# A Trainium2 backbone layer: x scaled by 1/rms while the modulation weights load, and a plain first tile in both feed-forwards

## Chip, cores and metric

One core of one Trainium2 chip. The metric is device time in microseconds (us), the median of several runs. A profile of one execution stands beside it, with its own time.

## What is computed

One layer of a diffusion backbone on 1024 latent tokens `x` and 256 context tokens `ctx`, width 1024, all in float32:

```python
m_x = silu(c) @ w_ada + b_ada          # nine modulations of 1024 for x; m_c from c_ctx for the context
x = x + 0.5 * m_x[2] * swiglu(modulate(rmsnorm(x, norm1_g), m_x[0], m_x[1]), ff1_in, ff1_out)
h = h + 0.5 * m_c[2] * swiglu(modulate(rmsnorm(h, norm1_g), m_c[0], m_c[1]), ff1_in, ff1_out)
x = x + m_x[5] * mixer(modulate(rmsnorm(x, norm2_g), m_x[3], m_x[4]), context states from h)
x = x + 0.5 * m_x[8] * swiglu(modulate(rmsnorm(x, norm3_g), m_x[6], m_x[7]), ff2_in, ff2_out)
return rmsnorm(x, final_g)
```

`modulate(x, shift, scale)` is `x * (1 + scale) + shift`; `swiglu` has 2816 hidden columns. The mixer joins gated linear attention and a spatial gate, and an output projection follows.

## The kernel before

Activations lie transposed: 8 tiles of 128 channels, `x[k][tb]`, with tb = 0 and 1 for two blocks of 512 tokens of x and tb = 2 for the context. Every precise product is made of three fp32r products (`hi*hi`, `hi*lo`, `lo*hi`); `hl` (L439 on) splits an operand into a high part on ScalarE (ACT) and a low part on VectorE (DVE). A plain fp32 matmul shows as two passes in the trace.

The big feed-forward products use a Winograd scheme over 2x2 blocks (`winograd`, L481 on): seven products (1 to 7) where plain blocks need eight. The right-hand operands `mov[1..7]` come from the four blocks of the normalized x: 1 and 2 are the upper and lower channels of the first token block; 5, 7, 6, 3 and 4 need the second block too. Each product is 12 instructions of 512 columns (L492); the context's part (`gc`, L539 to L541) has 256 columns. The weights of a tile f come through `unit` (L371 on): two loads into `raw` (two buffers), combinations on DVE, high and low parts in buffers with the tags `w` (six) and `m` (eight).

**The opening** (`run`): x of block 0 is loaded, then `ada_first` loads sixteen 512 KB tiles of modulation weights and multiplies each with two conditioning vectors into four PSUM banks (`row`, L206, two output rows each), copies them (L214) and turns them into columns with small products (`cols`, L216). Then come x of block 1 and the context. `rstd` squares on ACT (L305, L314), adds the eight squares up on DVE (L315), sums over channels with one-column products (`st`, L266) and takes 1/sqrt in 12 small DVE steps (L248 to L256, L280), once for each of the three blocks. `spread` (L289) copies 1/rms to all partitions by products into a PSUM bank `bc` (tag `pn`, two banks). `right_ops` (L447 on) multiplies x by its coefficient and by `bc` on DVE (L453), adds the shift on ACT (L454), and makes the operands. All this happens after the coefficients are known, block by block.

**Between the mixer and the second feed-forward** the mixer's last projection (`wo`, L357 to L360) adds to x one token block at a time; `done2(tb)` then normalizes that block and calls `right_ops`.

The order on each engine is set by the framework from the program's order, a simulated timeline and `high_priority` marks; each engine works its queue in that order. Loads go through SyncE's queue (SP).

Of the kernel before, what the change touches and what calls it, by code (L numbers as in the profile page):

```python
# [26 lines left out]
class Layer:  # L27
# [175 lines left out]
    def ada_rows(self, src, pr, i):  # L203
        wt = self.load(src[i], tag="d")
        for h in range(2):
            self.nc.tensor.matmul(pr[h][:2], self.sc[:, i, :], wt[:, h * 512:h * 512 + 512],  # L206
                                  start=(i == 0), stop=(i == NK - 1))

    def ada_cols(self, ch, pr):
        nc = self.nc  # L210
        row = self.m("row")
        pt = self.po("cols")
        for h in range(2):
            nc.scalar.activation(row[:2, h * 512:h * 512 + 512], pr[h][:2], AF.Copy)  # L214
            for dt in range(4 * h, 4 * h + 4):
                nc.tensor.matmul(pt[:, 2 * dt:2 * dt + 2], row[:2, dt * P:(dt + 1) * P], self.ident[:2, :2],  # L216
                                 start=True, stop=True)
        self.ada_bias(ch, 2, pt[:, :2 * NK].rearrange("p (k j) -> p k j", j=2))

    def ada_first(self):  # L220

        pr = [[self.po("row") for _ in range(2)], [self.pg("row") for _ in range(2)]]
# [61 lines left out]
    def spread(self, y, nt):  # L284

        nc = self.nc
        bc = self.pn("bc")
        for t in range(nt):
            nc.tensor.matmul(bc[:, t * P:(t + 1) * P], y[:, t:t + 1].to_broadcast([P, P]), self.ident,  # L289
                             start=True, stop=True)  # L290
        return bc
# [154 lines left out]

    def right_ops(self, tb, coef, bc, mov):  # L447

        nc = self.nc
        A, B = coef  # L450
        for k in (0, 4, 1, 5, 2, 6, 3, 7):
# [4 lines left out]
        def out(i, b, k):  # L456
            t = self.hl(b)
            mov[i][k] = t[:, :512], t[:, 512:]

        for k in range(4):  # L460
            if tb == 0:
                out(1, self.x[k][0], k)
                out(2, self.x[k + 4][0], k)
            else:
                (b11, b12), (b21, b22) = self.x[k][:2], self.x[k + 4][:2]
                self.combos(b11, b12, b21, b22, lambda i, b: out(i, b, k))
# [14 lines left out]
    def winograd(self, jobs):  # L481
# [24 lines left out]

        first(0)
        for j, job in enumerate(jobs):
            a, c, f = banks.pop(j), self.pg("c"), self.po("f")
            prod(c, job, 5)  # L510
            prod(f, job, 7)
            prod(a, job, 6, more=True)
            job[3].mid(a, c, f)
            if j + 1 < len(jobs):
                first(j + 1)
            prod(c, job, 3, more=True)
            prod(f, job, 4, more=True)
            job[3].end(c, f)

    def ffn(self, mov, yc, w1, w2, gates, load_x, load_c, tail, done, after_out=None):  # L520
# [14 lines left out]
        def plain(ps, parts, moving):  # L535

            n = len(parts)
            for i, ((hi, lo, c), (mh, ml)) in enumerate(zip(parts, moving)):
                nc.tensor.matmul(ps, hi[:, c], mh, start=i == 0, stop=False)  # L539
                nc.tensor.matmul(ps, hi[:, c], ml, start=False, stop=False)  # L540
                nc.tensor.matmul(ps, lo[:, c], mh, start=False, stop=i == n - 1)  # L541

        class Hidden:
# [3 lines left out]
            def ctx(s, i):  # L547
                w = s.w()
                rows = [(*w[r], slice(k * P, k * P + P)) for r in ((1, 2), (0, 4))[i] for k in range(4)]
# [3 lines left out]
                plain(ps, rows, yc)  # L553
# [9 lines left out]
                nc.sync.dma_start(hc[s.f // 2, :, h:h + 512], o.bitcast(F32))  # L563

# [63 lines left out]
        class Out:  # L628
# [4 lines left out]
            def ctx(s):  # L633
                w = s.w()
                ps = layer.po("oc")
                for i in range(2):
                    rows = [(*w[r], slice(s.col + k * P, s.col + k * P + P)) for r in ((1, 2), (0, 4))[i]
                            for k in range(s.kd)]
                    plain(ps[:, i * 256:i * 256 + 256], rows, s.right()["ctx"])
# [62 lines left out]
        def last():  # L702
# [3 lines left out]
                     for i in range(2)]  # L706
            rows = lambda w, i, col: [(*w[r], slice(col + k * P, col + k * P + P)) for r in ((1, 2), (0, 4))[i]
                                      for k in range(kd)]
            for tb in range(2):
# [6 lines left out]
                for m, i, w, col in tiles:  # L716
                    dt = m + 4 * i
                    ps = self.po("o") if i else self.pg("o")
                    plain(ps, rows(w, i, col), right)
# [8 lines left out]
            if yc:  # L728
# [6 lines left out]
                for m, i, w, col in tiles:  # L735
# [4 lines left out]
                    plain(ps, rows(w, i, col), right)  # L740
# [33 lines left out]
        self.winograd(jobs)  # L774
# [545 lines left out]
    def mixer(self, y, done=None):  # L1320
# [21 lines left out]
        for dt in range(NK):  # L1342
            w = self.wo_half(dt, 1, self.w)
            for tb in range(2):
                self.wo_add(w, bm[tb], dt, tb)
        ws = []
        ag = [self.gla_out(on[tb], tb) for tb in range(2)]
        for tb in range(2):
# [4 lines left out]
            if done:  # L1353
                done(tb)
# [22 lines left out]
    def run(self):  # L1377
# [11 lines left out]
        self.right_ops(0, c1, self.spread(rs[0], 4), mov)  # L1389
        y = ({}, {})  # L1390
        self.alloc_y(y, 2)
        self.norm(part(2), c1, y, rs[2])
        self.right_ops(1, c1, self.spread(rs[1], 4), mov)
# [23 lines left out]
        self.ffn(mov, yc, a["ff1i"], a["ff1o"], gates1, load_x1, lambda: self.load_c(self.d), self.squares(accs),  # L1417
# [16 lines left out]
        self.mixer(y2, done2)  # L1434
# [27 lines left out]
        self.ffn(mov, None, a["ff2i"], a["ff2o"], gates2, load_x2, None, self.squares(accs),  # L1462
# [81 lines left out]
```

## Time and profile before

| | |
|---|---|
| median of 3 runs | 2159.13 us (2155.48 to 2160.04) |
| the profiled execution | 2155.53 us, span 2153.8 us |
| TensorE (PE) busy | 2015.6 us, 94% |
| VectorE (DVE) busy | 1503.2 us, 70% |
| ScalarE (ACT) busy | 816.5 us, 38% |
| GpSimd (POOL) busy | 379.9 us, 18% |
| granted TensorE clock, mean | 0.968 |

Times in the profile count from the span's start. PE is the matmuls, PEld the weight loads beside them; matmuls are pipelined, so that the start of one after another tells their cost better than their length. A granted clock of 1.00 is 2.4 GHz, 0.50 is 1.2 GHz. In brackets stands how long an engine was idle before an instruction and what ended that.

### The profile page before, as it was taken

The numbers are of one execution on the slowest core, as the hardware profiler recorded it, in microseconds if no ns is written. First come the engines' busy times: TensorE is split into PE (matmuls) and PEld (weight loads), VectorE is DVE, ScalarE is ACT, GpSimd is POOL, SyncE is SP. The second block draws the span as 40 slices with busy tenths as digits, with TensorE's granted clock in tenths as the row PEclk, the third lists the DMA queues.
The fourth block names the chain that finished last, engine by engine and source line by source line (L and its number), as shares of the span: only waits on it lengthen the run. The fifth ranks groups of instructions, "written<-read, shape, count | busy, mean of one in ns | idle before, by whom it ended". The sixth has DMA issues, their size and how long they took to land.

```text
span 2153.8 us, 28445 instructions
## 1 busy us (share of the span) xinstructions
PE 2015.6 (94%) x10868; PEld 1669.6 (78%) x10868; DVE 1503.2 (70%) x2503; ACT 816.5 (38%) x1297; POOL 379.9 (18%) x215
## 2 busy tenths in 40 slices
PE   6799999999999999898999998787999999999997
PEld 1678888888887888787788877565888888868875
DVE  3976665656655779869888377778677786755585
ACT  3643333333333121256456345325343444442111
POOL 0000000000025555223210010300000000065740
PEclk9799999999999999999999899897999999999998
DMA  7033333333368786321111126550444343458742
GB/s 286 25 127 118 123 142 118 122 118 118 118 222 340 275 295 240 147 79 54 49 56 50 35 91 219 200 183 28 166 158 165 112 181 137 182 216 350 306 143 79
DMA packets 111273, 332.27 MB, mean 154 GB/s; under 512 B 12448, under 2 KB 15392, under 8 KB 111136
## 3 DMA queue, kind: packets, MB, share of 16 engines
q1 hardware_dynamic: 111136, 330.45, 41.8%
q8 instruction: 85, 1.39, 0.3%
q14 instruction: 52, 0.43, 0.1%
HBM read 231.31 MB, written 99.09 MB: 153 GB/s over the span
## 4 chain that ended last, share of the span: by engine, by line
PE 72%; DVE 18%; DMA 5%; issue 2%; ACT 2%; POOL 0%; SPq 0%; DVEq 0%; ACTq 0%
PE c L492 14%; PE a L492 14%; PE f L492 14%; PE b L492 7%; DVE acc L791 3%; DMA ar<-in_wb 2%; PE gc L541 2%; PE gc L540 2%; PE gc L539 2%; PE row L206 1%; DVE hl L444 1%; PE o L541 1%; PE o L539 1%; PE o L540 1%; DVE junk L169 1%
## 5 line engine op out<-in xcount | busy, mean ns | idle before, releaser
L384 POOL TENSOR_TENSOR s<-raw 128x512 f32<-128x512 f32 x18 | 23.8, 1322 | 1149.0 <-DVE ch L526 602.0
L169 DVE SCALAR_TENSOR_TENSOR junk<-ar,cr 128x512 bf16<-128x512 f32 x160 | 112.5, 703 | 58.6 <-DMA ar<-in_wb 44.1
L390 ACT ACTIVATE gh<-raw 128x1024 fp32r<-128x1024 f32 x62 | 65.7, 1059 | 171.6 <-PE c L492 64.1
L492 PE MATMUL f<-hl,uh 128*128 128x512 f32 x528 | 126.8, 389 | 0.0
L443 ACT ACTIVATE hl<-g 128x512 fp32r<-128x512 f32 x106 | 64.3, 626 | 157.4 <-DVE g L526 153.0
L492 PE MATMUL a<-hl,gh 128*128 128x512 f32 x352 | 114.4, 403 | 8.8 <-ACT hl L443 6.3
L492 PE MATMUL c<-hl,sh 128*128 128x512 f32 x352 | 111.1, 393 | 11.7 <-ACT hl L443 9.6
L394 ACT ACTIVATE sh<-s 128x1024 fp32r<-128x1024 f32 x62 | 65.5, 1057 | 147.1 <-PE a L492 87.1
L492 PEld LDWEIGHTS f<-hl,uh 128*128 128x128 f32 x528 | 99.1, 188 | 20.6
L492 PE MATMUL b<-hl,gh 128*128 128x512 f32 x352 | 112.3, 396 | 0.8 <-ACT hl L443 0.8
L492 PE MATMUL a<-hl,sh 128*128 128x512 f32 x352 | 110.1, 393 | 1.0 <-ACT g L567 1.0
L492 PE MATMUL f<-hl,th 128*128 128x512 f32 x352 | 110.2, 390 | 0.8 <-ACT hl L443 0.8
L492 PE MATMUL c<-hl,th 128*128 128x512 f32 x352 | 108.9, 391 | 0.0
L526 DVE TENSOR_TENSOR u<-c,u 128x512 f32<-128x512 f32 x44 | 30.2, 687 | 109.0 <-ACT u L577 109.0
L791 DVE SCALAR_TENSOR_TENSOR acc<-z,par,acc 128x945 f32<-128x945 f32 (+2 forms) x64 | 93.1, 1477 | 11.6 <-ACT acc L813 10.5
L143 POOL TENSOR_TENSOR wl<-raw,wh 128x1024 fp32r<-128x1024 f32 x20 | 52.0, 2606 | 257.5 <-ACT wh L142 257.2
L444 DVE TENSOR_TENSOR hl<-g,hl 128x512 fp32r<-128x512 f32 x106 | 74.9, 724 | 26.1 <-ACT hl L443 26.0
L492 PEld LDWEIGHTS c<-hl,sh 128*128 128x128 f32 x352 | 66.4, 189 | 27.4 <-ACT hl L443 10.2
L385 DVE TENSOR_TENSOR sl<-s,sh 128x1024 fp32r<-128x1024 f32 x44 | 54.8, 1246 | 45.2 <-PE gc L540 21.9
L492 PEld LDWEIGHTS a<-hl,gh 128*128 128x128 f32 x352 | 67.1, 195 | 23.0 <-ACT hl L443 6.8
L492 PEld LDWEIGHTS b<-hl,gh 128*128 128x128 f32 x352 | 67.3, 191 | 15.8 <-ACT hl L443 1.8
L492 PEld LDWEIGHTS a<-hl,sh 128*128 128x128 f32 x352 | 66.6, 189 | 15.7 <-ACT g L567 1.3
(342 smaller groups left out, 6030.6 us busy)
## 6 DMA issues: line engine op xcount, KB each, us to landing
hd<-hl SPq DMA_DIRECT2D x142, 512.0 KB, 3.6
hc<-hd SPq DMA_DIRECT2D x142, 512.0 KB, 7.4
ar<-in_wb SPq DMA_DIRECT2D x112, 256.0 KB, 3.1
raw<-in_ff1i SPq DMA_DIRECT2D x44, 512.0 KB, 3.7
raw<-in_ff2i SPq DMA_DIRECT2D x44, 512.0 KB, 4.5
raw<-in_ff1o SPq DMA_DIRECT2D x22, 512.0 KB, 4.9
raw<-in_ff2o SPq DMA_DIRECT2D x22, 512.0 KB, 4.8
x<-in_xT SPq DMA_DIRECT2D x16, 512.0 KB, 6.8
```

The source lines that it names most:

```text
L143: eng.tensor_tensor(out=lo[:, :n], in0=src[:, :n], in1=hi[:, :n].bitcast(F32), op=ALU.subtract)
L169: i = nc.vector.scalar_tensor_tensor(out=self.junk, in0=w, scalar=1.0, in1=cbc[j], op0=ALU.mult, op1=ALU.mult, accum_out=acc[:, h, dt, j:j ...
L385: sub = lambda o, x, y: eng.tensor_tensor(out=o, in0=x, in1=y, op=ALU.subtract)
L390: nc.scalar.activation(gh, g, AF.Copy)
L394: nc.scalar.activation(sh, s, AF.Copy)
L443: nc.scalar.activation(t[:, :512], src, AF.Copy)
L444: nc.vector.tensor_tensor(out=t[:, 512:], in0=src, in1=t[:, :512].bitcast(F32), op=ALU.subtract)
L492: mm = lambda x, y, start, stop: nc.tensor.matmul(ps, x, y, start=start, stop=stop, skip_group_check=more)
L539: nc.tensor.matmul(ps, hi[:, c], mh, start=i == 0, stop=False)
L540: nc.tensor.matmul(ps, hi[:, c], ml, start=False, stop=False)
L541: nc.tensor.matmul(ps, lo[:, c], mh, start=False, stop=i == n - 1)
L791: self.nc.vector.scalar_tensor_tensor(out=o, in0=zv[:, r0 + dr:r1 + dr, c0 + dc:c1 + dc], scalar=self.par[:, tap:tap + 1], in1=o, op0=ALU. ...
```

## The change

Four parts:

1. In `run` all of x and the context is loaded first, then the weights `w0` of the first feed-forward tile (`halves`, split at once), then the sixteen modulation weight tiles. While these load, `scaled` makes the squares of all three blocks, sums them with one-column products straight from the squares (only block 1 is added up on DVE first), takes 1/rms in one chain for all ten columns, spreads it and multiplies x by it in place.
2. In `ada_first` the rows' products go to one bank, in four groups of 32 partitions, and are ordered behind the last product of the spreading. The copies of the rows are split between ACT and DVE and ordered behind the last multiplication of x. The turn into columns uses four banks.
3. `right_scaled` makes the operands from the scaled x: scale and shift in one ACT instruction, operands 1, 2, 5, 3 first, then 7, 6, 4; operand 5 from the difference of the two blocks, which needs no shift. `right_ops`, kept for the second feed-forward, gets the same order.
4. The first tile of each feed-forward is computed plainly, with eight products for seven: `block0` needs operands 1 and 2 alone, then come products 1 and 2 of the next tile, then `block1` (operands 5 and 3). Its weights need no combinations. In the second feed-forward they are loaded and split (on POOL) ahead of the last projection's second group of weights.

```diff
-    def ada_first(self):
...
+    def ada_first(self, order):
+        nc = self.nc
+        pr = self.pg("row")
+        wts = [[self.load(self.a["wa"][ch, i], tag="d") for ch in range(2)] for i in range(NK)]
+        mm, order = order()
         for i in range(NK):
             for ch in range(2):
-                self.ada_rows(self.a["wa"][ch], pr[ch], i)
+                for h in range(2):
+                    g = 32 * (2 * ch + h)
+                    self.after(mm, nc.tensor.matmul(pr[g:g + 2], self.sc[:, i, :], wts[i][ch][:, h * 512:h * 512 + 512],
+                                                    start=(i == 0), stop=(i == NK - 1)))
+        row = self.h("row")
+        pts = [self.po("cols"), self.pg("cols"), self.po("cols"), self.pg("cols")]
         for ch in (1, 0):
-            self.ada_cols(ch, pr[ch])
+            for h in range(2):
+                q = 2 * ch + h
+                r = slice(32 * q, 32 * q + 2)
+                i = nc.scalar.activation(row[r], pr[r], AF.Copy) if h else nc.vector.tensor_copy(row[r], pr[r])
+                self.after(order, i)
+                for dt in range(4):
+                    nc.tensor.matmul(pts[q][:, 2 * dt:2 * dt + 2], row[r, dt * P:(dt + 1) * P], self.ident[r, r],
+                                     start=True, stop=True)
...
+    def right_scaled(self, coef, mov):
...
+        for k in range(4):
+            ds.append(self.h("dx"))
+            nc.vector.tensor_tensor(out=ds[k], in0=x[k][0], in1=x[k][1], op=ALU.subtract)
+        for k in range(4):
+            for i, kk in ((1, k), (2, k + 4)):
+                self.shift(x[kk][0], coef, kk)
+                self.right_op(mov, i, k, x[kk][0])
+        for k in range(4):
+            t = self.d("hl", F32R)
+            n = na[:, k:k + 1]
+            nc.scalar.activation(t[:, :512], ds[k], AF.Identity, scale=n)
+            nc.vector.scalar_tensor_tensor(out=t[:, 512:], in0=ds[k], scalar=n, in1=t[:, :512].bitcast(F32),
+                                           op0=ALU.mult, op1=ALU.subtract)
+            mov[5][k] = t[:, :512], t[:, 512:]
+        for k in range(4):
+            self.shift(x[k + 4][1], coef, k + 4)
+            self.right_op(mov, 3, k, x[k + 4][1])
...
+        plain.block0()
         first(0)
+        plain.block1()
...
+            def block0(s):
+                w = s.w()
+                s.pq = layer.w("pq")
+                a, b = layer.pg("a"), layer.po("b")
+                for ps, (i, j), c in ((a, (1, 2), 0), (b, (0, 4), 512)):
+                    plain(ps, rows(w, (i,)), mov[1])
+                    nc.scalar.activation(s.pq[:, c:c + 512], ps, AF.Copy)
+                    plain(ps, rows(w, (j,)), mov[2], True)
...
+            def block1(s):
+                w = s.w()
+                c, f = layer.pg("c"), layer.po("f")
+                for ps, rs in ((c, (1, 2)), (f, (0, 4))):
+                    plain(ps, rows(w, rs), mov[5] + mov[3])
...
-        for f in range(NF):
-            w = lazy(w1[f], nc.vector)
+        for f in range(1, NF):
+            w = lazy(w1[f], nc.vector, self.m if f == 1 else None)
...
-        self.load_x(0, new)
-        self.ada_first()
-        self.load_x(1, new)
-        self.load_x(2, [self.m])
-        rs = [self.rstd(part(0)), self.rstd(part(1)), self.rstd(part(2))]
+        for tb in range(3):
+            self.load_x(tb, new if tb < 2 else [self.m])
+        w0 = self.halves(a["ff1i"][0], nc.vector, self.w)
+        y = ({}, {})
+
+        def scaled():
...
+                    nc.scalar.activation(sqs[k], self.x[k][tb], AF.Square)
+                    if tb == 1 and k:
+                        nc.vector.tensor_tensor(out=sqs[0], in0=sqs[0], in1=sqs[k], op=ALU.add)
+                if tb == 1:
+                    sqs = sqs[:1]
+                for t in range(n // P):
+                    for k, sq in enumerate(sqs):
+                        nc.tensor.matmul(st[:, 4 * tb + t:4 * tb + t + 1], sq[:, t * P:(t + 1) * P], self.ones[:, 0:1],
+                                         start=(k == 0), stop=(k == len(sqs) - 1))
+            r = self.rstd_cols([None] * 5, 256, 1.0 / 1024.0, None, st)
+            for tb in range(3):
+                n = TBS[tb][1]
+                bc, mm = self.spread(r[:, 4 * tb:4 * tb + n // P], n // P, True)
+                for k in range(NK):
+                    i = nc.vector.tensor_tensor(out=self.x[k][tb], in0=self.x[k][tb], in1=bc[:, :n], op=ALU.mult)
+            return mm, i
+
+        self.ada_first(scaled)
...
+        def weights2():
+            late["w0"] = self.halves(a["ff2i"][0], nc.gpsimd, self.w)
```

## Rows read from the trace of the kernel before

**Rows 1.** The chain that ended last, in order of time: start, length, what.

```profile
16.34 25.84 PE row L206 x60
...
1531.52 5.44 PE a L492 x24
```

**Rows 2.** The timeline of TensorE in the opening: start, length, instruction.

```profile
82.26 0.55 PE L539 MATMUL gc<-y,gh 128*128 128x256 f32 x1 [7.79 <-ACT x L454]
...
86.66 0.33 PE L541 MATMUL gc<-y,gl 128*128 128x256 f32 x1
...
90.07 0.28 PE L539 MATMUL gc<-y,vh 128*128 128x256 f32 x1
90.19 0.28 PE L540 MATMUL gc<-y,vh 128*128 128x256 f32 x1
```

**Rows 3.** Busy time by stretch: length; PE, PEld, DVE, ACT, POOL; granted clock; DMA.

```profile
42.00:46.00 4.00, 3.84 (x33) 3.64 (x32) 1.71 (x4) 4.00 (x9) 0.00 (x0) 0.97 0.02 4
46.00:62.00 16.00, 4.76 (x20) 4.41 (x20) 14.38 (x37) 7.47 (x15) 0.00 (x0) 0.50 0.20 66
...
1316.00:1318.00 2.00, 2.00 (x21) 2.00 (x21) 0.29 (x2) 0.00 (x0) 0.00 (x0) 0.50 0.37 108
```

**Rows 4.** The same of one line's products (L492, L539, L492): PE, PEld.

```profile
62.00:120.00 58.00, 29.84 (x106) 20.54 (x107) 0.85 0.08 25
...
62.00:120.00 58.00, 10.03 (x32) 7.04 (x32) 0.85 0.08 25
...
1449.00:1510.00 61.00, 37.50 (x122) 26.98 (x123) 0.80 0.11 41
```

**Rows 5.** The timeline of TensorE on the way into the second feed-forward.

```profile
1455.30 0.64 PE L492 MATMUL a<-hl,gh 128*128 128x512 f32 x1 [3.43 <-ACT hl L443]
...
1478.20 0.79 PE L492 MATMUL c<-hl,sh 128*128 128x512 f32 x1 [9.14 <-ACT hl L443]
```

**Rows 6.** The timeline of all engines in the opening.

```profile
9.29 2.39 ACT L314 ACTIVATE sq<-x 128x512 f32<-128x512 f32 x4 [0.68 <-DMA x<-in_xT]
...
11.94 3.42 PE L206 MATMUL row<-raw,sc 128*2 128x512 f32 x4 [11.94 <-DMA raw<-in_wa]
...
15.29 1.05 PE L266 MATMUL st<-ones,acc 128*128 128x1 f32 x8
...
16.38 0.16 DVE L280 TENSOR_SCALAR r<-st 128x4 f32<-128x4 f32 x1 [3.34 <-PE st L266]
...
18.55 0.16 DVE L256 SCALAR_TENSOR_TENSOR r<-r 128x4 f32<-128x4 f32 x1
...
31.86 0.63 ACT L305 ACTIVATE acc<-x 128x512 f32<-128x512 f32 x1 [20.18 <-DMA x<-in_xT]
...
48.16 0.17 DVE L231 SCALAR_TENSOR_TENSOR A<-mods,par 128x16 f32<-128x16 f32 x1
...
54.07 1.87 PE L266 MATMUL st<-ones,acc 128*128 128x1 f32 x8 [8.23 <-DVE acc L315]
...
57.92 2.05 PE L289 MATMUL bc<-ident,r 128*128 128x128 f32 x8
```

**Rows 7.** Instructions by line and shape, 0 to 130 us: busy, mean ns, idle before.

```profile
L444 DVE TENSOR_TENSOR hl<-x,hl 128x512 fp32r<-128x512 f32 x20 | 13.4, 683 | 0.0
L443 ACT ACTIVATE hl<-x 128x512 fp32r<-128x512 f32 x20 | 12.2, 622 | 2.4 <-DVE x L427 2.3
...
L454 ACT ACTIVATE x<-x,mods 128x512 f32<-128x512 f32 x16 | 10.8, 717 | 7.2 <-DVE x L453 7.1
```

**Rows 8.** The timeline of TensorE in the gate mixing of the mixer.

```profile
1315.77 3.50 PE L1280 MATMUL mix<-wst,vs 128*64 128x128 f32 x31
```

**Rows 9.** The page's costliest groups: weight splits on DVE and POOL.

```profile
L143 POOL TENSOR_TENSOR wl<-raw,wh 128x1024 fp32r<-128x1024 f32 x20 | 52.0, 2606 | 257.5 <-ACT wh L142 257.2
...
L385 DVE TENSOR_TENSOR sl<-s,sh 128x1024 fp32r<-128x1024 f32 x44 | 54.8, 1246 | 45.2 <-PE gc L540 21.9
```

**Rows 10.** The timeline of DVE on the way into the second feed-forward.

```profile
1500.18 1.29 DVE L444 TENSOR_TENSOR hl<-x,hl 128x512 fp32r<-128x512 f32 x2
```

More of the change, by code (lines that the diff above doesn't have):

```diff
@@ L445, in hl, with right_op, shift, t2 @@
         return t
+    def right_op(self, mov, i, k, b):
+        t = self.hl(b)
+        mov[i][k] = t[:, :512], t[:, 512:]
+    def shift(self, x, coef, k, j=0):
+        A, B = coef
+        self.nc.scalar.activation(x, x, AF.Identity, scale=A[:, k, j:j + 1], bias=B[:, k, j:j + 1])
+    def right_scaled(self, coef, mov):
+        nc = self.nc
+        A = coef[0]
+        na = self.const([P, NK], "na")
+        nc.vector.tensor_scalar(out=na, in0=A[:, :, 0], scalar1=-1.0, scalar2=None, op0=ALU.mult)
+        x = self.x
+        ds = []
+        for k in range(4):
[15 more added lines that the diff above has]
+            self.right_op(mov, 3, k, x[k + 4][1])
+        def t2(k):
+            nc.vector.scalar_tensor_tensor(out=ds[k], in0=ds[k], scalar=A[:, k, 0:1], in1=x[k + 4][1],
+                                           op0=ALU.mult, op1=ALU.add)
+            return ds[k]
+        for k in range(4):
+            self.shift(x[k][1], coef, k)
+        self.right_last(mov, t2)
+    def right_last(self, mov, t2):
+        tt = lambda o, x, y: self.nc.vector.tensor_tensor(out=o, in0=x, in1=y, op=ALU.subtract)
+        for k in range(4):
+            (b11, b12), (b21, b22) = self.x[k][:2], self.x[k + 4][:2]
+            tt(b12, b22, b12)
+            self.right_op(mov, 7, k, b12)
+            t = t2(k)
+            self.right_op(mov, 6, k, t)
+            tt(b21, b21, t)
+            self.right_op(mov, 4, k, b21)
     def right_ops(self, tb, coef, bc, mov):
@@ L450, in right_ops, with norm @@
         A, B = coef
-        for k in (0, 4, 1, 5, 2, 6, 3, 7):
+        tt = lambda o, x, y: nc.vector.tensor_tensor(out=o, in0=x, in1=y, op=ALU.subtract)
+        def norm(k):
             x = self.x[k][tb]
@@ L533, in ffn, with plain, rows @@
         pairs0 = NF // 2 - CHUNKS[-1]
-        def plain(ps, parts, moving):
+        def plain(ps, parts, moving, more=False):
             n = len(parts)
+            mm = lambda x, y, a, b: nc.tensor.matmul(ps, x, y, start=a, stop=b, skip_group_check=more)
             for i, ((hi, lo, c), (mh, ml)) in enumerate(zip(parts, moving)):
-                nc.tensor.matmul(ps, hi[:, c], mh, start=i == 0, stop=False)
-                nc.tensor.matmul(ps, hi[:, c], ml, start=False, stop=False)
-                nc.tensor.matmul(ps, lo[:, c], mh, start=False, stop=i == n - 1)
+                mm(hi[:, c], mh, i == 0 and not more, False)
+                mm(hi[:, c], ml, False, False)
+                mm(lo[:, c], mh, False, i == n - 1)
+        def rows(w, rs):
+            return [(*w[r], slice(k * P, k * P + P)) for r in rs for k in range(4)]
         class Hidden:
@@ L552, in ctx @@
                 ps = s.pc[:, i * 256:i * 256 + 256]
-                plain(ps, rows, yc)
+                plain(ps, rows(w, ((1, 2), (0, 4))[i]), yc)
                 if i == 0:
@@ L636, in ctx @@
                 for i in range(2):
-                    rows = [(*w[r], slice(s.col + k * P, s.col + k * P + P)) for r in ((1, 2), (0, 4))[i]
-                            for k in range(s.kd)]
-                    plain(ps[:, i * 256:i * 256 + 256], rows, s.right()["ctx"])
+                    parts = [(*w[r], slice(s.col + k * P, s.col + k * P + P)) for r in ((1, 2), (0, 4))[i]
+                             for k in range(s.kd)]
+                    plain(ps[:, i * 256:i * 256 + 256], parts, s.right()["ctx"])
                 for i in range(2):
@@ L706, in last @@
                      for i in range(2)]
-            rows = lambda w, i, col: [(*w[r], slice(col + k * P, col + k * P + P)) for r in ((1, 2), (0, 4))[i]
-                                      for k in range(kd)]
+            parts = lambda w, i, col: [(*w[r], slice(col + k * P, col + k * P + P)) for r in ((1, 2), (0, 4))[i]
+                                       for k in range(kd)]
             for tb in range(2):
@@ L718, in last @@
                     ps = self.po("o") if i else self.pg("o")
-                    plain(ps, rows(w, i, col), right)
+                    plain(ps, parts(w, i, col), right)
                     more(self.x[dt][tb], ps, dt, 0)
@@ L739, in last @@
                     ps = pc[:, i * 256:i * 256 + 256]
-                    plain(ps, rows(w, i, col), right)
+                    plain(ps, parts(w, i, col), right)
                     more(self.x[dt][2], ps, dt, 1)
@@ L1387, in run @@
+        self.ada_first(scaled)
+        self.alloc_y(y, 2)
         c1 = self.norm_coef(0, C_N1, 2, "1")
         mov = {i: [None] * 4 for i in range(1, 8)}
[L1389 to L1393, printed above, removed]
+        for k in range(NK):
+            hi, lo = y[0][2][k], y[1][2][k]
+            x = self.x[k][2]
+            self.shift(x, c1, k, 1)
+            nc.scalar.activation(hi, x, AF.Copy)
+            nc.vector.tensor_tensor(out=lo, in0=x, in1=hi.bitcast(F32), op=ALU.subtract)
```

95 lines of the change are left out of this document (57 added, 38 removed).

## The prediction, made before the changed kernel was run

> **What bounds the kernel now.** The page was read first: TensorE counts as busy nearly everywhere, so a gain has to come from the places where it waits or runs at its lower clock. The chain that ended last and the tables by stretch showed two: the opening, up to 120 us, and the way into the second feed-forward, 1449 to 1510 us; their timelines were read next. In the opening the chain first holds the products of the modulation rows, 60 passes in 25.84 us [rows 1]; behind them it is mostly DVE until the first feed-forward runs at full pace. In full swing 24 products of 512 columns take 5.44 us, 0.227 us each [rows 1], and products of 256 columns follow each other every 0.12 us [rows 2]. The granted clock is 0.97 while the rows are turned into columns and 0.50 right after [rows 3].
>
> I measure a place by its lost time: its length less what its products would take at full pace. Up to 120 us there are 106 products of 512 columns and 96 of 256 (32 on each of three lines, one shown) [rows 4]: 106 x 0.227 + 96 x 0.12 = 35.6 us of work, so **84.4 us are lost**. In the second place 61 us hold 122 products [rows 4], 27.7 us of work: **33.3 us lost**; the longest wait in it is 9.14 us, for a split of a late right-hand operand [rows 5].
>
> **The opening after the change.** Ten transfers of 512 KB (x and the context) are issued first, then two of w0, then the sixteen of the modulation weights. Before, the fifth was used at 11.94 us and the 21st at 31.86 [rows 6]: 19.92/16 = 1.25 us each. So the tenth lands at 18.2 and the 28th at 40.7. That w0 goes ahead of the modulation weights on SP's queue costs them 2.5 us, hidden as long as the rows' products can't start before 40.7.
>
> When they can start is a new chain:
> - The sums of squares become 32 + 4 + 16 = 52 products of one column, because two of the three blocks lose DVE's adds. Each is two passes; eight passes took 1.05 us at full clock (0.12 with the tail off) and 1.87 at half (0.22) [rows 3, 6]. I take half: the array starts there (the first four passes of rows took 3.42 us, later ones 0.43 each [rows 1, 6]), and after the 32 passes of two columns, in which TensorE was busy throughout, the clock was down at once [rows 3]. Eight products go with the first block's squares, which end at 11.7 [rows 6]; the other 44 need 19.6: **31.3**. By the Trainium skill ("TensorE: Matmul & The Clock Gate", LDWEIGHTS) a weight load takes its columns at 1.2 GHz, an estimate of 0.107 us for these, and names no lower clock. The rows here differ by two between the clocks and decide.
> - One rsqrt chain, 16.38 to 18.71 in the old one [rows 6]: 33.7. Spreading the first block, eight passes, 2.05 at half clock [rows 6]: 35.8. The third block's spreading needs a bank that the first block's eight multiplications give back (there are two): 8 x 0.61 on DVE, whose operations of this size take 683 ns with some 0.08 overlapped [rows 7], then four passes, 1.0: **41.7**. Behind this wait stand all rows' products on TensorE, and everything after them.
> - Rows' products: still 64 passes of 0.43, 27.5 us in all, now in four column groups of one bank. That such groups overlap shows in the gate mixing, 128 columns in two groups: 31 passes in 3.50, the last 0.47 of it a tail, 0.10 each at clock 0.50 [rows 3, 8], against 0.244 for the undivided spreading of as many columns at that clock [rows 6]: 2.4 times. So 11.5, plus 1.7 for the first four at half clock: **54.9**. The bounds are one at a time (27.5) and four at a time (6.9).
> - From the rows' end to the coefficients it was 42.2 to 48.3 [rows 1, 6]. The copies now alternate between ACT and DVE; I take 5, plus 0.8 for the first shift and split of the context: first product at 60.7. The multiplications of x by 1/rms (24) lie beside the rows' products and end near 48 on DVE.
> - From there TensorE has enough in hand: the context, 48 products of the plain tile that need only the first block, the next tile's 24, then 48 that need two more operands. ACT makes two operands in 2.3 us (717 and 622 ns, 0.1 of each overlapped, twice [rows 7]); TensorE uses them in 12 x 0.227 = 2.7. The first 4.4 us run at half clock, as from 82.26 to 86.66 [rows 2]: 2.2 lost. For waits on weights I allow 3, two splits of 1.25 [rows 9] and their signals. The second tile's low parts need buffers of which w0 holds four of six; they come free halfway through the last 48 products, and the 24 after that (5.4 us) cover two splits. Without that cover it would be 2.5 more.
>
> Lost: 60.7 + 2.2 + 3 = 66. The plain tile has eight products for seven: 12 instructions, 2.7 us. **84.4 - 66 - 2.7 = 15.7 us gained.** Bounds: 27 with the sums at full clock, about 0 with the rows one at a time.
>
> **The second place.** DVE's work hardly changes: it ends with the last split at 1501.47 [rows 10]. What changes is how much TensorE can do meanwhile. From the first block alone it has 48 + 24 products, where 24 stood before the wait of 9.14 us; then 48 as the fifth and third operands come, which are now made first. Up to 1501.5 it can do all but the last twelve products of two tiles, and the next tile's 24: 192, 43.6 us, and with 2.2 for a slow start this fits between the first product at 1455.3 [rows 5] and 1501.5. From 1449 that is 8.9 lost; I add a second fall of the clock (2.2), the allowance of 3 for weights and another 3 for operands that come late in a queue kept in order: 17. **33.3 - 17 - 2.7 = 13.6, taken as 13.** Bounds: -2.7 (the time isn't used) and 22. The new weight load puts two transfers on SP and two splits on POOL (2.6 us by the nearest row [rows 9]) ahead of the last projection's eight loads; the products of the gate mixing's half of that projection lie over them. Without that cover: 2 x (1.25 + 2.6) = 8.
>
> What is left of the diff renames. **Sum: 28.7 us.** The profiled execution took 2155.5, so 2126.8; it lies 3.6 below the median of the runs, and 2126.8 + 3.6 = **2130** compares with that.
>
> **Rivals.**
> 1. The sums of squares run at full clock. For it: they are one unbroken stream; against: [rows 3]. They then end 16 x 0.24 after the last square (19.5), at 23.4, the spreading at 32, the rows at 43.6, close to the last transfer. 11 us more: 2119. The weight load of 0.107 us by the Trainium skill ("TensorE: Matmul & The Clock Gate", LDWEIGHTS) would make about the same.
> 2. The rows' products take turns, so that part of the change doesn't do what it says. For it: no row has 512 columns in four groups; against: the mixing. They end at 70.9: 2146. The Trainium skill ("TensorEngine Tiling (Array Packing)", Theoretical Speedup) speaks for overlap, up to four times, which would be 4.6 us better than my sum.
> 3. DVE stays the bound in the second place, and products kept in order stand behind late operands again. For it: the chain there is DVE's. The 13 are gone and the plain tile costs 2.7: 2146. With rival 2 as well: 2162, which can't be told from no change.
> 4. Slower: the rows' products take turns and stay at half clock, in which the sums before them left the array. A pass then costs 0.85 us, they end at 96.1 instead of 54.9, and the time is 2171. This mechanism decides the sign from a pass of (13.2 + 28.7)/64 = 0.65 us. Against: before, these products were at full clock after four passes [rows 6].
>
> **How the numbers follow.** Forecast 0.45, rival 1 0.14, rival 2 0.11, rival 3 0.12, 2 and 3 together 0.08, rival 4 0.10. About 0.2%, 4.3 us, can be told from no change. Faster: 0.45 + 0.14 + 0.11 + 0.12 = 0.82; same 0.08; slower 0.10. The range goes from rival 1 with a better second place (2119 - 7 = 2112) to rivals 2 or 3 with the two covers gone (2146 + 2.5 + 8 = 2157); the two cases left out hold 0.18.
>
> **What would show it.** Right: passes of the sums at 0.22 us and ending near 31, the last spreading near 42, rows' passes at some 0.18 us and ending near 55, dense products from 61 on without a wait over 3 us, and in the second place no wait of 9 us and a loss near 17. Wrong: a rows' pass of 0.43 or more, a last spreading well past 42, or TensorE waiting for the second tile's weights.

## The result and the profile after

The median went to **2139.1 us** (four runs, 2135.9 to 2140.8), beside 2157.3 for the kernel before on the same chip: a ratio of 0.9916, with a 95% interval of 0.9893 to 0.9939. That is 18.2 us faster; 28.7 were forecast. The sign and the range were right, the size was not. The profiled execution took 2140.7 us (span 2138.9).

TensorE in the opening of the changed kernel, from its timeline (start, us, then what it waited for); these lines answer to [rows 1, 2, 6]:

```profile
10.97 19.88 PE L1510 MATMUL st<-ones,sq 128*128 128x1 f32 x92 [0.18 <-ACT sq L1503]
33.37 3.78 PE L292 MATMUL bc<-ident,r 128*128 128x128 f32 x16 [2.51 <-DVE r L259]
40.49 1.19 PE L292 MATMUL bc<-ident,r 128*128 128x128 f32 x4 [3.35 <-DVE x L1517]
41.62 9.31 PE L214 MATMUL row<-raw,sc 128*2 128x512 f32 x64
...
65.16 0.58 PE L609 MATMUL gc<-y,vh 128*128 128x256 f32 x1 [7.42 <-ACT y L1528]
...
73.99 0.58 PE L609 MATMUL gc<-y,vh 128*128 128x256 f32 x1 [3.16 <-ACT y L1528]
```

The sums end at 30.85, the last spreading at 41.7, the rows at 50.9: all as forecast or better. Then comes a hole of 14 us with only the small transpositions in it, and a second hole at 71 to 74. ScalarE's timeline in the first hole:

```profile
51.73 0.59 ACT L222 ACTIVATE row<-row 2x512 f32<-2x512 f32 x1 [7.42 <-DVE row L222]
54.97 0.59 ACT L222 ACTIVATE row<-row 2x512 f32<-2x512 f32 x1 [2.65 <-DVE row L222]
57.09 2.07 ACT L457 ACTIVATE c<-c,mods,A 128x256 f32<-128x256 f32 x4 [1.54 <-DVE mods L228]
59.07 5.73 ACT L457 ACTIVATE x<-x,mods,A 128x512 f32<-128x512 f32 x8
64.71 1.01 ACT L1528 ACTIVATE y<-c 128x256 fp32r<-128x256 f32 x3
```

VectorE's timeline there:

```profile
51.01 0.69 DVE L222 COPY row<-row 2x512 f32<-2x512 f32 x1 [2.02 <-PE row L214]
51.73 2.49 DVE L469 TENSOR_TENSOR dx<-x,x 128x512 f32<-128x512 f32 x4
54.26 0.68 DVE L222 COPY row<-row 2x512 f32<-2x512 f32 x1
```

ScalarE's copies of the rows wait for VectorE's copies into the same tile; four block differences (`dx`) stand between VectorE's two copies; and ScalarE shifts four chunks of context and eight of x before it makes the first split (writing the high part, `y`). The windows of the same kernel (length; busy time of PE, PEld, DVE, ACT, POOL; granted clock; DMA):

```profile
51.00:65.00 14.00, 4.63 (x32) 4.45 (x32) 4.68 (x12) 9.08 (x15) 0.00 (x0) 0.57 0.01 2
65.00:82.00 17.00, 13.45 (x57) 12.15 (x58) 13.16 (x24) 17.00 (x34) 0.00 (x0) 0.65 0.11 31
82.00:120.00 38.00, 38.00 (x187) 32.16 (x186) 29.90 (x47) 19.66 (x34) 0.00 (x0) 1.00 0.20 63
```

Up to 120 us TensorE ran 156 products of 512 columns (96 of line 609, 60 of line 561) and 86 of 256: 156 x 0.227 + 86 x 0.12 = 45.7 us of work, so 74.3 us are lost (the time beyond that work), where 66 were forecast and 84.4 were lost before.

The second place is the way into the second feed-forward. On TensorE the first block's spreading follows the projection's end at once (this answers to [rows 5]):

```profile
1435.78 1.05 PE L292 MATMUL bc<-ident,r 128*128 128x128 f32 x8
1445.14 0.79 PE L609 MATMUL a<-hl,vh 128*128 128x512 f32 x1 [8.32 <-ACT hl L446]
...
1473.22 0.79 PE L609 MATMUL c<-hl,vh 128*128 128x512 f32 x1 [2.63 <-DVE hl L447]
```

The wait of 9.14 us in the middle is gone, and one of 8.32 stands in front, where 3.43 stood before. In the 61 us behind the last `wo` TensorE ran 162 products instead of 122: 24.2 us lost instead of 33.3, where 17 were forecast.

And there is a change in a part that the diff doesn't touch. TensorE's waits from the mixing to the end of the output projection, in us, times and the longest; before, 1310 to 1450 us:

```profile
PE wo L357 <- DVE x L1372: 19.5, 13, 11.6
```

After, 1290 to 1440 us:

```profile
PE wo L360 <- DVE x L1476: 10.0, 6, 3.7
```

The projection's results can be added to x only when the residual's gate is known, a sum over modulation weights that VectorE makes piece by piece. The last piece of the sum and the instruction that completes it, in VectorE's timeline of before:

```profile
1351.10 0.69 DVE L169 SCALAR_TENSOR_TENSOR junk<-ar,cr 128x512 bf16<-128x512 f32 x1 [5.15 <-DMA ar<-in_wb]
...
1353.61 0.17 DVE L155 TENSOR_TENSOR mods<-acc,par 128x8 f32<-128x8 f32 x1
```

And of after:

```profile
1335.10 0.15 DVE L155 TENSOR_TENSOR mods<-acc,par 128x8 f32<-128x8 f32 x1
```

Before, VectorE stood 5.15 us waiting for that piece's weights: in SP's queue the last transfers of the sum (`ar<-in_wb`) stood among those that bring back x and the gated output's input, issued from 1332.6 us on. After, fourteen of them were issued in a row up to 1331.1, ahead of these.

Starts of products of the same tiles in the profiled executions (us, one execution each; the experiments are explained below) show where the time came from. `oc` belongs to the end of the first feed-forward (the context's output), `glr` is the mixer's first product, `mix` its gate mixing, `wo` the output projection behind it, `o` the output of the second feed-forward:

| | first `oc` | first `glr` | last `mix` | last `wo` | last `o` |
|---|---|---|---|---|---|
| before | 627.0 | 952.7 | 1327.4 | 1449.0 | 2134.3 |
| after | 619.6 | 946.6 | 1326.8 | 1435.5 | 2118.6 |
| e1 second Winograd | 618.5 | 945.2 | 1326.3 | 1433.9 | 2126.6 |
| e2 first Winograd | 625.1 | 951.2 | 1334.9 | 1446.0 | 2131.5 |
| e3 rows in turn | 633.8 | 958.7 | 1335.8 | 1447.2 | 2131.0 |
| e4 opening order | 612.1 | 937.3 | 1323.1 | 1434.2 | 2118.2 |
| e5 second alone | 630.4 | 954.3 | 1331.2 | 1454.3 | 2132.6 |
| e6 gate too early | 630.4 | 953.9 | 1364.1 | 1455.8 | 2139.5 |
| e7 rows free | 619.1 | 943.9 | 1325.4 | 1433.5 | 2113.9 |
| e9 gate before | 630.5 | 954.7 | 1334.2 | 1445.3 | 2132.9 |
| e8 sums and order | 605.6 | 929.1 | 1304.4 | 1439.4 | 2121.0 |
| e10 gate and opening | 606.4 | 929.8 | 1305.3 | 1418.5 | 2102.3 |
| e11 e10, rows free | 608.3 | 932.2 | 1312.2 | 1423.7 | 2108.3 |
| e12 second order | 605.3 | 931.3 | 1303.5 | 1417.8 | 2102.7 |

After against before: 7.4 won up to `oc`, 1.3 given back up to `glr` and 5.5 between `glr` and the last `mix`, 12.9 won in the projection, 2.2 behind it. The 5.5 are not settled: before, e5 and e9, with the mixer's old order but for the gate, took 374.7 to 379.5 us there, the changed kernel 380.2. The 12.9 can't be read alone either, for a mixing that ends later leaves a shorter projection (e6): over mixer and projection together, 7.4 us are won.

### The profile page after: what moved, and what is told of

Read it like the earlier page. It is cut to its first block, busy times and chain, and to the rows that moved or that the text cites. A ratio compares the mean times of both kernels' runs of the same rounds, so it can differ in the third digit from the quotient of the medians.

```text
span 2138.9 us, 28608 instructions
## 1 busy us (share of the span) xinstructions
PE 2021.9 (95%) x10976; PEld 1697.3 (79%) x10976; DVE 1479.5 (69%) x2449; ACT 816.0 (38%) x1298; POOL 384.7 (18%) x217
## 4 chain that ended last, share of the span: by engine, by line
PE 73%; DVE 13%; DMA 6%; ACT 3%; issue 3%; POOL 1%; SPq 0%; DVEq 0%; ACTq 0%; POOLq 0%
PE a L561 14%; PE c L561 14%; PE f L561 14%; PE b L561 7%; PE gc L609 6%; DVE acc L895 3%; PE o L609 3%; PE oc L609 3%; DMA ar<-in_wb 2%; DVE acc L597 2%; DVE x L790 1%; DMA hc<-hd 1%; DVE junk L169 1%; PE st L1510 1%; PE st L269 1%
## 5 line engine op out<-in xcount | busy, mean ns | idle before, releaser
L561 PE MATMUL f<-hl,uh 128*128 128x512 f32 x504 | 121.1, 389 | 0.0
L561 PE MATMUL a<-hl,gh 128*128 128x512 f32 x336 | 105.4, 393 | 0.0
L561 PE MATMUL b<-hl,gh 128*128 128x512 f32 x336 | 104.7, 391 | 0.0
L561 PE MATMUL c<-hl,sh 128*128 128x512 f32 x336 | 104.0, 390 | 0.0
L561 PE MATMUL c<-hl,th 128*128 128x512 f32 x336 | 104.0, 391 | 0.0
L561 PE MATMUL f<-hl,th 128*128 128x512 f32 x336 | 103.6, 389 | 0.3 <-ACT th L400 0.3
L561 PE MATMUL a<-hl,sh 128*128 128x512 f32 x336 | 103.8, 389 | 0.0
L895 DVE SCALAR_TENSOR_TENSOR acc<-z,par,acc 128x945 f32<-128x945 f32 (+2 forms) x64 | 93.1, 1476 | 11.6 <-ACT acc L917 10.5
L609 PE MATMUL o<-hc,vh 128*128 128x512 f32 x256 | 80.4, 395 | 0.5 <-DVE acc L597 0.5
L675 ACT ACTIVATE g<-g 128x512 f32<-128x512 f32 x42 | 26.5, 631 | 125.1 <-DVE g L597 125.1
L561 PEld LDWEIGHTS f<-hl,th 128*128 128x128 f32 x336 | 63.0, 188 | 13.8 <-ACT th L400 0.8
```

Source lines behind the costliest of these rows:

```text
L609: mm = lambda x, y, a, b: nc.tensor.matmul(ps, x, y, start=a, stop=b, skip_group_check=more)
L675: nc.scalar.activation(s.g0, s.g0, AF.Silu)
L895: self.nc.vector.scalar_tensor_tensor(out=o, in0=zv[:, r0 + dr:r1 + dr, c0 + dc:c1 + dc], scalar=self.par[:, tap:tap + 1], in1=o, op0=ALU. ...
```

## The experiments

Ratios are to the kernel before on the same chip, with their 95% intervals. The edits are shown shortened.

**e1: the second feed-forward's first tile as seven products.**
```diff
-late["w0"] = self.halves(a["ff2i"][0], nc.gpsimd, self.w)
+late["w0"] = None      # ffn: tiles from 0, no plain one
```


> Only the second feed-forward's first tile goes back to seven products (its weights' loads and splits at the mixer's end are gone with it); all else as after the change. Theory A (the plain tile lets TensorE start on one block): before the change TensorE waited 9.14 us there for the second block's splits; that wait comes back, less the 2.7 us that the plain tile's 12 extra products cost, so some 6 us slower than the changed kernel: 2145 us. Theory B (VectorE bounds that stretch either way, with the plain tile or without): the 2.7 us are saved and nothing comes back: 2136 us. Beside it: if the 6 us that the mixer lost between its first and last products came from the early load of these weights, they are won back here (end of the mixing products at 1321 instead of 1327 us); if they came from the shifted opening, that end stays at 1327.

0.9954 (0.9941 to 0.9967): 8 us slower than the changed kernel, theory A. A wait for a split is back, and the stretch from the last `wo` to the last `o` takes 692.7 instead of 683.1 us.

```profile
1465.66 0.79 PE L561 MATMUL c<-hl,sh 128*128 128x512 f32 x1 [9.93 <-ACT hl L446]
```

The mixing ends at 1326.3, so the early load of these weights is not what the mixer lost; and the projection ends as early as in the changed kernel, so the plain tile is not what it won.

**e2: the first feed-forward's first tile as seven products.** The same edit for `ff1i`.

> Only the first feed-forward's first tile goes back to seven products (and its early weights' loads and splits are gone); the scaled opening and the second feed-forward stay as after the change. Theory A: the products that need one block alone (24 of 512 columns, 48 of 256 for the context) are done near 88 us and the last splits of the second block come near 97 to 100 us, so TensorE waits 8 to 11 us, less 2.7 us of work saved: 2145 us. Theory B: the context's products and the scheduler's freedom fill the gap, only the 2.7 us are saved: 2136 us.

0.9952 (0.9934 to 0.997): the time of theory A, not its mechanism. TensorE shows no wait for the second block's splits; it started 4 us later (69.2 us), `oc` came 5.5 us later, and mixer and projection took 5.9 us more than in the changed kernel. What the plain tile is worth here stays open.

**e3: the rows one at a time.**
```diff
-nc.tensor.matmul(pr[g:g + 2], self.sc[:, i, :], ...
+nc.tensor.matmul(pr[ch][h][:2], self.sc[:, i, :], ...
```


> The modulation rows' 64 passes write four banks at partitions 0 and 1, as before the change, instead of four groups of columns of one bank. Theory A (passes on different column groups overlap): 64 passes in turn at 0.43 us are 27.5 us instead of 9.31 us, so the opening ends 18 us later: 2157 us. Theory B (what bounds the rows is the transfers of their weights and the spreading, not the products): less than 3 us: under 2142 us.

0.9990 (0.9976 to 1.0003), theory A: nearly the whole gain is gone. Its timeline:

```profile
41.33 29.50 PE L213 MATMUL row<-raw,sc 128*2 128x512 f32 x64
```

29.50 us instead of 9.31: passes in four column groups of one bank overlap 3.2 times, beside passes in turn in four banks. `oc` comes 14.2 us later.

**e4: another order in the opening.**
```diff
-row = self.h("row")
+both = self.h("row"), self.sv("row")      # VectorE's, ScalarE's
...
+self.after(last_split, shift); self.after(na, dx)
```


> The changed kernel with another order in the opening: the row copies of VectorE and of ScalarE go to two tiles and don't wait for one another, the four block differences come behind the coefficients, ScalarE shifts and splits the context chunk by chunk first, then x the same way, instead of four context shifts, eight x shifts, and so on. Theory A (the first product waits for the order of ScalarE and VectorE, not for their sum): first product near 56 instead of 65.16 us, the first block's splits done 6 to 7 us earlier: 2132 us. Theory B (the total of ScalarE's and VectorE's work up to the first tile's end, or the half clock of scattered products, sets the end): first product early, but the wait comes back behind the context's products: 2137 to 2139 us.

0.9890 (0.9864 to 0.9915), a median of 2132.6 us. In the opening it is theory A:

```profile
51.84 4.08 PE L227 MATMUL cols<-ident,row 2*128 2x2 f32 x32 [0.82 <-DVE row L224]
57.98 0.58 PE L613 MATMUL gc<-y,vh 128*128 128x256 f32 x1 [2.07 <-ACT y L1532]
```

The first product comes 7.2 us earlier, and `oc` 7.5. So half of the 14 us between the rows and the first product was order alone. That these 7 us reach the end is not shown: the interval overlaps that of the changed kernel, and in the profiled execution, the slowest of the four with 2139.7 us, they are given back in mixer and projection (496.9 us instead of 488.9).

**e5: the second place alone,** on the kernel before.

> The kernel before with the second feed-forward's part of the change alone: its first tile plain, its weights early, the new order of norms and splits there; the opening and the first feed-forward as before the change. The mixer keeps the old order of instructions, so the wait of 11.6 us for the residual's gate at the head of the output projection stays as in the kernel before. Theory A (the plain tile gives what putting it back took away, 7 us in the median and 9.6 us in the profiled stretch): some 7 us faster than before. Theory B (the prediction's 13 us): 13 us faster. Theory C (the plain tile only catches the backlog that an earlier end of the projection leaves on VectorE, so nothing is won without that earlier end): within 2 us of before.

0.9985 (0.9971 to 0.9999), 3 us. From the last `wo` to the last `o` it took 678.3 us instead of 685.3: the second place gives 7.0 by itself, as theory A says, and some 4 of it don't arrive, in a mixer (first `glr` to last `mix`) and a projection that took 2.2 and 1.5 us more than in the row of before.

**e6: the gate's sums moved ahead of the second block's attention,** on the kernel before.

> The kernel before with one thing moved: the sixteen partial sums of the residual's gate in the mixer stand ahead of the second block's gated attention instead of behind it; nothing of the change is in it. In the changed kernel the gate was ready at 1335.1 us, before it at 1353.6 us, and TensorE's wait for it fell from 11.6 us to nothing, though no line of that part was changed. Theory A (that shift of the schedule is worth its wait): the output projection ends 10 to 12 us earlier and the kernel is some 11 us faster than before. Theory B (VectorE's backlog, which the projection leaves behind, holds the first block's norm and splits): the projection ends earlier, but TensorE then waits in front of the second feed-forward, and the kernel is 2 to 5 us faster.

1.0006 (0.9992 to 1.002). Too early: the gate was complete at 1203.2, but the mixing ended at 1364.1 instead of 1327.4 (that those sums held up VectorE's part of the attention is argued, not shown), and the projection behind it took 91.7 us instead of 121.6. Both theories had the projection's end earlier; it ended at 1455.8. This says nothing of the order at issue; e9 and e10 do.

**e7: the rows not held behind the spreading.**
```diff
-self.after(mm, nc.tensor.matmul(pr[g:g + 2], ...))
+nc.tensor.matmul(pr[g:g + 2], ...)
```


> The changed kernel without the order that puts the rows' products behind the spreading of 1/rms: the rows' products then stand in TensorE's queue as their weights come, twenty of the thirty-two pairs ahead of the first two spreads, the last spread behind all rows. Theory A (the order pays): the spreads wait for weights, x is scaled 4 to 8 us later, the first product comes later than 65.16 us by as much: 2144 us. Theory B (the order costs: rows end near 43 instead of 50.93 us and that counts more): first product 3 to 6 us earlier, 2134 us. Theory C: the two cancel, 2137 to 2141 us.

```profile
31.00 5.98 PE L214 MATMUL row<-raw,sc 128*2 128x512 f32 x40
36.91 2.05 PE L292 MATMUL bc<-ident,r 128*128 128x128 f32 x16
38.89 2.82 PE L214 MATMUL row<-raw,sc 128*2 128x512 f32 x20
41.96 1.03 PE L214 MATMUL row<-raw,sc 128*2 128x512 f32 x4 [0.25 <-DMA raw<-in_wa]
```

First product at 65.8, `oc` at 619.1: in the opening it cancels, as theory C says. The whole came to 0.9883 (0.9862 to 0.9905), a median of 2134.2 us, theory B's time without its mechanism; the interval overlaps that of the changed kernel, and of the 4.7 us that its last `o` comes earlier, 0.5 lie in the opening. The order is not what makes the change pay. The last line shows the last weights landing at 41.9 (the prediction had 40.7).

**e8: the order of e4, and all squares added up by VectorE** (10 one-column products instead of 52).
```diff
-if tb == 1 and k:
+if k:
...
-if tb == 1:
-    sqs = sqs[:1]
+sqs = sqs[:1]
```


> The other order of the opening as in the run before this one that had it (first product 58.0 us), and beside it the squares of all three blocks added up by VectorE, so that 10 one-column products make the sums instead of 52. Theory A (the one-column products at half clock hold the spreads): the sums end near 23 instead of 30.85 us, the last spread near 34, the rows' products come as their weights land and end near 43 instead of 50.9 us, first product near 51 us, some 7 us faster than with the order alone: 2126 us. Theory B (the weights' transfers, 40.7 us for the 28th, and the rows behind them set the end): the rows end no earlier than 48 us and less than 3 us are won: 2130 us or more.

In the opening theory A held, some 2 us late (sums' end 26.2, rows' end 45.2, first product 52.0), and the mixing ended 22.4 us before that of the changed kernel. Yet the ratio is 0.9913 (0.9889 to 0.9936), a median of 2140.6 us instead of the 2126 of theory A: nothing more than the change. Its waits from 1290 to 1440 us say where the time went:

```profile
PE wo L362 <- DVE x L1480: 31.9, 11, 21.5
```

The gate was complete at 1339.6, 35 us behind the last `mix`, although everything else was early. Ahead of its end VectorE stood 3.91 us waiting for weights of that sum, 2.34 for the gated output's input, and worked on the gated output.

**e9: the gate first,** on the kernel before, by an order on VectorE and one on SP's queue.
```diff
-self.nc.vector.tensor_tensor(out=ov, in0=ov, in1=on[h], op=ALU.mult)
+self.after(gate, self.nc.vector.tensor_tensor(out=ov, ...))
...
+self.after(gate_load, <loads of x and of the gated output's input>)
```


> The kernel before with one order added, and nothing of the change: VectorE's products of the gated output stand behind the sum that makes the residual's gate, and the transfers that bring back x and the gate's input stand behind the last weights of that sum; nothing is moved ahead of the attention this time. Theory A (the changed kernel's 13 us in the output projection come from this order alone, and reach the end): TensorE's wait of 11.6 us for the gate falls under 4 us, the projection ends some 10 us earlier than 1449.0 us, the kernel is 8 to 11 us faster than before. Theory B (they come from it, but the second feed-forward's start, which waits for VectorE, takes them back without the plain tile): the projection ends 10 us earlier, the kernel is 1 to 5 us faster. Theory C (the order isn't what moved it): the projection ends within 3 us of where it ended before.

0.9981 (0.9964 to 0.9997); the medians differ by 4.5 us. The waits, 1320 to 1446 us:

```profile
PE wo L359 <- DVE x L1374: 7.0, 5, 2.6
```

No theory fits whole. The wait for the gate is gone, as theory A has it, but the gate came only 4.8 us earlier (1348.8) and the mixing ended 6.8 us later, so that TensorE met the gate later too. The projection took 111.1 us instead of 121.6 and ended 3.7 us earlier, where A and B had 10 and C under 3. Over mixer and projection together it took 490.6 us instead of 496.3: 5.7 won, of the 7.4 of the changed kernel. The time is that of theory B: from the last `wo` to the last `o` it took 687.6 instead of 685.3, with a wait of 9.4 us for a split.

**e10: e8 with the gate first.**

> The changed kernel with the other opening (order and sums of squares, as in the run that combined them) and the same order for the residual's gate as in the run beside this one. That combined run started its feed-forward 13 us earlier than the changed kernel, ended the mixing products 22 us earlier, and lost all of it in a wait of 21.5 us for the gate. Theory A (the scheduler had put the gate's sum behind the gated output; nothing else holds the projection): that wait falls under 5 us, the projection ends near 1420 instead of 1439.4 us, the kernel comes to 2122 us. Theory B (VectorE and the transfers of the residual hold the projection whatever stands first): it ends no earlier than 1432 us, 2134 us or more.

**0.9845 (0.9827 to 0.9864), a median of 2126.1 us: faster than both kernels.** Theory A:

```profile
PE wo L364 <- DVE x L1482: 7.9, 4, 3.2
```

Beside e8 this is the clean test of the gate's two orders: the mixing ends at the same time (1305.3 beside 1304.4), the gate is complete at 1322.9 instead of 1339.6, the projection ends at 1418.5 instead of 1439.4, and the intervals of the two ratios lie apart. How much of it is VectorE's order and how much that of the transfers was not tried.

**e11: e10 with the rows free.**

> As the run with the other opening and the gate's order, and the rows' products not held behind the spreading. Theory A (the rows' products now stand in front of the last spread and wait there for weights that land up to 40.7 us, so x of the context is scaled later; with the sums already early this costs): 0 to 4 us slower than the run beside it. Theory B (TensorE has room there, the rows end earlier by what the last spread waits): first product 2 to 4 us earlier than 52.0 us and the kernel as much faster.

0.9854 (0.9829 to 0.9878), first product at 54.6: not better, theory A.

**e12: e10 with another order on VectorE in the second place.**
```diff
+self.after(los[-2], norm)      # norms two ahead of the splits
...
+self.after(last_split, <sums of the next tile's weights>)
```


> The best version so far (other opening, gate first) with two orders in the second feed-forward: the norms of x stand two ahead of the splits instead of eight in a row, and VectorE's sums for the next tile's weights stand behind the first block's splits. There, as in the changed kernel (8.32 us), TensorE stood idle between the projection's end at 1418.5 us and the first product at 1432.6 us but for 16 short passes. Theory A (what kept the second place from giving the forecast 13 us is the order of VectorE's queue: 3.5 us of weight sums and 5.35 us of norms ahead of the first split): the first product comes 8 to 10 us behind the projection's end instead of 14, and the end of the output products comes 678 us behind it instead of 683.8: 2120 us. Theory B (VectorE's total there is the bound; what is put behind is missed by the second tile): the first product is earlier, and the wait comes back in front of the second tile's products, 683 us as before: 2126 us.

0.9860 (0.9833 to 0.9886). The first product comes 5.1 us behind the projection's end instead of 14.1, and the stretch to the last `o` takes 684.9 us instead of 683.8. Theory B in its times. Windows of e10 (columns as above):

```profile
1420.00:1460.00 40.00, 26.68 (x103) 21.34 (x104) 31.76 (x69) 25.54 (x44) 0.00 (x0) 0.75 0.14 48
1460.00:1500.00 40.00, 39.59 (x165) 31.96 (x164) 35.02 (x53) 17.20 (x28) 0.00 (x0) 0.95 0.17 66
```

Windows of e12:

```profile
1420.00:1460.00 40.00, 30.65 (x122) 22.23 (x122) 34.64 (x65) 25.20 (x41) 0.00 (x0) 0.91 0.20 70
1460.00:1500.00 40.00, 34.35 (x131) 26.11 (x131) 32.54 (x49) 19.20 (x31) 0.00 (x0) 0.91 0.12 39
```

TensorE does 19 instructions more in the first 40 us and 34 fewer in the next, where it now waits for splits one by one. In the 80 us behind the last `wo` VectorE is busy for 66.4 us in both kernels. That its total work is the bound is likely, not shown: it also stands idle here until the second block's 1/rms is spread, by products in TensorE's own queue, for 5.31 us in e10, 3.70 in e12 and 6.77 in the changed kernel:

```profile
1461.81 5.35 DVE L513 SCALAR_TENSOR_TENSOR x<-x,A,bc 128x512 f32<-128x512 f32 x8 [6.77 <-PE bc L292]
```

In the changed kernel that spreading starts at 1460.71, while its input was ready at 1455.0. An order that moves it forward was not tried.

## Why the prediction was partly right

**Sums, spreading, rows: right.** Sums end at 30.85 us (31.3 forecast), the chain of rsqrt at 33.3 (33.7), the last spreading at 41.7 (41.7). Rival 1 is out. The rows were better than the sum: 0.145 us a pass and an end at 50.9 instead of 54.9, because the overlap is 3.2 times and not the 2.4 taken from two groups. Rivals 2 and 4 are out, and e3 shows what rival 2 would have cost: nearly the whole gain.

**From the rows' end to the first product: the step that failed.** "I take 5, plus 0.8 for the first shift and split" made 5.8; it was 14.2, of which 6.2 up to the coefficients. The 0.8 assumed that ScalarE would make the first split as soon as the coefficients were there; the scheduler put twelve shifts in front of it, 7.6 us. e4 took 7.2 of the 14.2 away by order alone. The term for the half clock, 2.2, was too small too: the clock averaged 0.65 up to 82 us, with a second wait of 3.16 in it. The better rows made up 4 of this. Lost up to 120 us: 74.3 instead of 66; after the 2.7 for the plain tile the opening gave 7.4 instead of 15.7, the same 7.4 that `oc` shows.

**The second place: half of the term.** 13 forecast; by itself it gives 7.0 (e5), and putting the old tile back costs 9.6 in that stretch (e1). By the prediction's own measure the changed kernel gives 33.3 - 24.2 - 2.7 = 6.4 here. The wait of 9.14 us did go, as forecast. What failed is "up to 1501.5 it can do all": the first product waits for VectorE, which brings the next tile's sums and a norm before the first split, and all eight norms before the first low part. The one other order that was tried (e12) doesn't win it back. That fits rival 3, VectorE as the bound, though not to the point of taking all; the wait for the second block's spreading stands beside it, untested.

**What the forecast didn't have.** The scheduler orders the mixer anew for every kernel, and in the changed one the weights of the residual's gate went ahead of the returned x in SP's queue. The gate was complete 8.3 us behind the last `mix` instead of 26.2. It comes with the new opening: in e1 it is 8.3 too, in e5, with the old opening, 24.2. Not every early opening does it: in e8 it is 35.2. TensorE's wait of 11.6 us went with it, and mixer and projection together took 7.4 us less. That the gate's place can do this, e10 beside e8 shows; on the kernel before, its order alone gave 5.7 there and 4.5 at the end (e9; by its interval 0.6 to 7.8). Whether the mixer's 5.5 us are order or spread stays open: e9's mixer took 4.8 us more as well, e10's, beside e8, only 0.2.

So the total fell nearer to the forecast than its two terms, and that was luck: 28.7 were forecast for the opening and the second place, which measure 7.4 and some 6.4 to 7; the gate, in no term, brought several us more. The second place's gain doesn't all arrive: at the last `o` 2.2 are left, and the other 4 are lost behind 1497 us, where TensorE's longer waits come to 13 us instead of 10 and the clock is 0.96 for 40 us; the cause wasn't tried.

## What to carry to other kernels

After a change in one stage, look at the order that the scheduler gives to all later ones: a gain of 14 us in the opening was wholly lost in a single wait of 21.5 us more than a thousand microseconds later, and an order for a small sum and its transfers brought it back. Between the last input and the first product, count what the queue of the engine holds in front of the first operand, not the operand's own cost. Where one engine is busy for most of a stretch, another order can move the wait without shortening it, as in e12.

## What the runs showed of the hardware

Products of two rows in four column groups of one bank overlapped 3.2 times: 64 passes of 512 columns in 9.31 us beside 29.50 in turn (e3). In the changed kernel's sums of squares each one-column pass took 0.216 us (92 in 19.88), and the spreading behind them 0.236 us for 128 columns (16 in 3.78); in the kernel before, eight one-column passes took 1.05 us at 15.29 [rows 6], and behind the changed kernel's projection eight passes of the spreading took 1.05. Yet the granted clock of those stretches reads 1.00:

```profile
0.00:31.00 31.00, 23.20 (x104) 22.79 (x104) 8.29 (x14) 15.31 (x28) 0.20 (x4) 1.00 0.94 362
31.00:42.00 11.00, 5.29 (x24) 4.52 (x28) 8.46 (x23) 0.00 (x0) 0.00 (x0) 1.00 1.03 410
```

The durations are near the 1.87 and 2.05 us for eight that such passes took where the clock read 0.50 [rows 3, 6], so here they fit the lower of the two clocks and the column doesn't show it. Why it doesn't is open.
